# The second feed-forward product by seven half products per 512 inner rows

## The chip, the core and the metric

One core of one Trainium2 chip. The metric is the device time of one execution in microseconds (us): TensorE does matmuls, VectorE (DVE), ScalarE (ACT) and GpSimd (Pool) do the rest, SyncE (SP) issues the weight transfers. A run is timed several times and its median is given.

## What is computed

One decoder layer for 512 tokens of width 2048: two groups of linear-attention heads, then a feed-forward part (FF) of inner width 8192. Of the reference only the last lines matter here:

```python
h = rmsnorm(x, pre_ffn_norm[l]) * (1.0 + sc_f) + sh_f
y = jnp.square(jax.nn.relu(h @ w_ff1[l])) @ w_ff2[l]
x = x + gt_f * rmsnorm(y, post_ffn_norm[l])
```

All data are float32. `w_ff1` is 2048 x 8192, `w_ff2` is 8192 x 2048.

## The kernel before

**Split products.** Each float32 operand is split into a high part (a cast to the fp32r type, on ScalarE) and a low part (the difference, on VectorE, rarely on Pool). A product is three matmuls (`mm3`): high x high, high x low, low x high, all into one PSUM bank of 128x512.

**The weight stream.** `WeightStream` walks a `plan`, a list of weight tiles of 128x1024 in the order of their use. `_load` issues the transfer of a tile into one of three `raw` buffers; `_split` makes `wh` (L81) and `wl` (L83) in one of two buffers each; `get` returns the split tile that is due, after it has issued loads three tiles ahead and splits one tile ahead. `on_get` is called at each `get`; in the FF it advances, at every third call, `ada_gtf`, which loads 64 tiles of `w_ada`, scales them on ScalarE (L320) and adds them on Pool (L322) to `gacc2`, the gain of the last norm.

**The FF.** The 8192 inner columns are done in `NR` = 16 rounds of 512. `ff1(r)` computes the round's 512 inner columns, as four blocks of 128 inner columns (on partitions) by 512 tokens: 8 weight tiles, 24 matmuls each, 4 PSUM banks (`pf`), then relu, square, cast (`gH`) and difference (`gL`). `ff2(r)` multiplies them with 512 rows of `w_ff2`: for each of four column blocks `nb` of 512, two weight tiles (`hf`), four token blocks, each in a bank (`pg`) that collects 12 matmuls; VectorE then copies (first round, L1480) or adds (L1482) the bank into `y2` in SBUF. The order is `ff1(0)`, `ff1(1)`, `ff2(0)`, `ff1(2)`, `ff2(1)` and so on. Inside this loop the instruction order of TensorE and SyncE is as written (`manual_schedule`); that of VectorE, ScalarE and Pool is chosen by the compiler's scheduler. After the loop the gain is summed over partitions (`total_of`, banks `pgf`), and `ff2(NR - 1)` and the last norm follow, the last two column blocks in a token-by-token order written out by hand for all engines.

**PSUM.** Eight banks: three `pj` (for `pf`), two `wg`, and `wh`, `sg`, `sh`. `ff2` uses `wg`, `wg`, `wh`, `sg`.

```python
with tc.manual_schedule(engines={ET.PE, ET.SP}):
    for r in range(NR):
        ff1(r)
        if r >= 1:
            ff2(r - 1)
```

Of the kernel before, what the change touches and what calls it, by code (L numbers as in the profile page):

```python
# [45 lines left out]
class WeightStream:  # L46


    def __init__(self, nc, pool, plan, load_ahead, split_ahead, bufs):
# [7 lines left out]
        self.raw, self.hl = {}, {}  # L57

    def _load(self):
        i = self.nl  # L60
        raw = self.pool.tile([P, 1024], F32, tag="raw", name=f"raw{i}", bufs=self.bufs[0])
        ap = self.plan[i][1]
# [5 lines left out]
        self.raw[i] = raw  # L68
        self.nl += 1
        if self.on_load is not None:  # L70
            self.on_load(1.46)

    def _split(self):
        i = self.ns
        raw = self.raw.pop(i)
        pool, nb = self.pool, self.bufs
        if len(self.plan[i]) > 2:
            pool, nb = self.alt, (0, self.plan[i][2], self.plan[i][2])
        h = pool.tile([P, 1024], F32R, tag="wh", name=f"wh{i}", bufs=nb[1])
        lo = pool.tile([P, 1024], F32R, tag="wl", name=f"wl{i}", bufs=nb[2])  # L80
# [3 lines left out]
        ap = self.plan[i][1]  # L84
        k = 8 if isinstance(ap, list) else ap.shape[1]
        self.hl[i] = (
            h.rearrange("p (k n) -> p k n", k=k),
            lo.rearrange("p (k n) -> p k n", k=k),
        )
        self.ns += 1  # L90

    def get(self, key):
        i = self.ng
        assert self.plan[i][0] == key, (self.plan[i][0], key)
        n = len(self.plan)
        while self.nl < min(n, i + 1 + self.la):
            self._load()
            while self.ns < min(self.nl, i + 1 + self.sa):
                self._split()
        while self.ns < min(n, i + 1 + self.sa):  # L100
# [8 lines left out]
def hybrid_layer_kernel(  # L109
# [68 lines left out]

    def plan_f1(r):
        for g in range(RB // 2):  # L180
            for q in range(4):
                plan.append((("f1", r * RB * P + g * 256, q), w256(W1, r * RB * P + g * 256, q)))

    def plan_f2(r):
# [4 lines left out]

    for r in range(NR):  # L190
        plan_f1(r)
        if r >= 1:
            plan_f2(r - 1)
    plan_f2(NR - 1)
# [22 lines left out]
    ws = WeightStream(nc, wpool, plan, 3, 1, (3, 2, 2))  # L217
    ws.pool_l = range(LP0, LP1, LP2)


# [1197 lines left out]
    with ExitStack() as st:  # L1418
        fp = st.enter_context(tc.tile_pool(name="ff", bufs=1))
        y2 = big.tile([P, 4, D], F32, tag="y", name="y2")  # L1420
        gacc2 = fp.tile([P, D], F32, tag="gacc", name="gacc2")
        gH, gL = {}, {}

        def ada_gtf():
# [3 lines left out]
            for i in range(4 * KT + 2):  # L1428
# [4 lines left out]
                if i >= 2:  # L1433
                    cb, r = divmod(i - 2, KT)
                    ada_pool(queue.pop(0), 512, r, 1, gacc2[:, cb * 512 : (cb + 1) * 512], False)
                yield

        def ff1(r):
            gH[r] = fp.tile([P, RB, T], F32R, tag="gH", name=f"gH{r}", bufs=2)
            gL[r] = fp.tile([P, RB, T], F32R, tag="gL", name=f"gL{r}", bufs=2)  # L1440
            for g in range(RB // 2):
                col = r * RB * P + g * 256
                pss_ = [pj(f"pf{col}_{cb}") for cb in range(2)]
                for q in range(4):
                    wH, wL = ws.get(("f1", col, q))
                    for cb in range(2):
                        for kk in range(4):
                            kt = q * 4 + kk
                            cs = slice(cb * P, (cb + 1) * P)
                            mm3(pss_[cb], wH[:, kk, cs], wL[:, kk, cs], h2H[:, kt, :], h2L[:, kt, :],  # L1450
                                kt == 0, kt == KT - 1)
                for cb in range(2):
                    j = g * 2 + cb
                    rl = fp.tile([P, T], F32, tag="rl", name=f"rl{r}_{j}", bufs=2)
                    nc.scalar.activation(out=rl, in_=pss_[cb], func=AF.Relu)
                    sq = fp.tile([P, T], F32, tag="sq", name=f"sq{r}_{j}", bufs=2)
                    nc.scalar.activation(out=sq, in_=rl, func=AF.Square)
                    nc.scalar.copy(out=gH[r][:, j, :], in_=sq)
                    nc.vector.tensor_tensor(out=gL[r][:, j, :], in0=sq, in1=gH[r][:, j, :].bitcast(F32),
                                            op=ALU.subtract)  # L1460

        FB = ("wg", "wg", "wh", "sg")

        def ff2_mm(ps, r, tok, hf, w):
            ts = slice(tok * P, (tok + 1) * P)
            for jj in range(2):
                j = 2 * hf + jj
                mm3(ps, gH[r][:, j, ts], gL[r][:, j, ts], w[0][:, jj, :], w[1][:, jj, :], j == 0, j == RB - 1)

        def ff2(r, nbs=range(4)):  # L1470
            for nb in nbs:
# [5 lines left out]
                for tok in range(4):  # L1477
                    dst = y2[:, tok, nb * 512 : (nb + 1) * 512]
                    if r == 0:
                        nc.vector.tensor_copy(out=dst, in_=ps4[tok])  # L1480
                    else:
                        nc.vector.tensor_tensor(out=dst, in0=ps4[tok], in1=dst, op=ALU.add)  # L1482

# [8 lines left out]
        ws.on_get = on_get  # L1492
        with tc.manual_schedule(engines={ET.PE, ET.SP}):
            for r in range(NR):
                ff1(r)
                if r >= 1:
                    ff2(r - 1)


        Gf = big.tile([P, D], F32, tag="hL", name="Gf")  # L1500
        nc.sync.dma_start(out=Gf, in_=post_ffn_norm[0].partition_broadcast(P))
        for cb in range(4):
            cs = slice(cb * 512, (cb + 1) * 512)
            ps = pj(f"pgf{cb}")
            total_of(ps, gacc2[:, cs], fp.tile([P, T], F32R, tag="rl", name=f"gfH{cb}", bufs=2),
                     fp.tile([P, T], F32R, tag="sq", name=f"gfL{cb}", bufs=2))
            nc.vector.tensor_tensor(out=Gf[:, cs], in0=ps, in1=Gf[:, cs], op=ALU.mult)
# [5 lines left out]
        rsf = fp.tile([P, 4], F32, name="rsf")  # L1513
        junk = fp.tile([P, 512], BF16, name="junkf")

        ws.alt = fp

# [10 lines left out]

        zl = fp.tile([P, 512], F32, name="zl")

# [66 lines left out]
```

## Time and profile before

| | us |
|---|---|
| median of 3 runs | 2715.55 (2712.93 to 2716.62) |
| the profiled execution | 2714.78 |
| its span, first to last instruction | 2713.1 |
| TensorE busy | 2563.6 (94%) |
| VectorE busy | 1440.6 (53%) |
| ScalarE busy | 1016.4 (37%) |
| Pool busy | 569.9 (21%) |

The span has three parts: the start and the heads, until about 1100 us; the output projection and norms, until about 1310 us; the FF. In the trace a matmul is shown longer (0.39 us) than the distance to the next, since neighbours overlap; distances between starts are what to read. The same holds for short instructions of VectorE in a row.

### The profile page before, as it was taken

To read this page: it belongs to the slowest core of one execution; us is meant where nothing else is said; L and a number is where in the kernel's file an instruction comes from. 1 tells how busy PE (TensorE), PEld (TensorE's weight loads), DVE (VectorE), ACT (ScalarE), POOL (GpSimd) and SP (SyncE) were. 2 spreads that over 40 slices of the span, in tenths; PEclk is the share of its full clock that TensorE was granted. 3 is DMA by queue.
4 is the path that set the end of the run, shared out by engine and by line. 5 is a ranking of instruction groups with operands and counts; after the bars stand their busy time and mean duration, and the time that the engine had idled before them with its cause. 6 is when DMAs were issued, how large, how long until landed. Compare 5 with 4: busy or idle time off the path is not lost.

```text
span 2713.1 us, 34048 instructions
## 1 busy us (share of the span) xinstructions
PE 2563.6 (94%) x12987; PEld 2080.2 (77%) x12987; DVE 1440.6 (53%) x2265; ACT 1016.4 (37%) x1675; POOL 569.9 (21%) x496
## 2 busy tenths in 40 slices
PE   5889999999997789999999999999999999999997
PEld 3667777777775567788788888888888888888886
DVE  7997868776865366634533343334333344334346
ACT  5543554454543242433533233332233223322233
POOL 4560344544444340000100000000000000000003
PEclk8999999999998899999999999999999999999999
DMA  9974885778899985445233333333333333332342
GB/s 280 283 186 73 133 138 128 151 138 153 139 138 103 98 135 79 143 129 186 90 117 109 118 112 115 111 114 111 112 117 111 115 110 116 105 101 93 101 171 109
DMA packets 335938, 350.65 MB, mean 129 GB/s; under 512 B 17191, under 2 KB 255001, under 8 KB 334621
## 3 DMA queue, kind: packets, MB, share of 16 engines
q1 hardware_dynamic: 335578, 348.42, 53.8%
q8 instruction: 102, 1.67, 0.2%
q14 instruction: 62, 0.51, 0.1%
q10 hardware_dynamic: 196, 0.06, 0.0%
HBM read 340.01 MB, written 8.40 MB: 128 GB/s over the span
## 4 chain that ended last, share of the span: by engine, by line
PE 65%; DVE 5%; DMA 3%; issue 2%; POOL 1%; ACT 1%; SPq 0%; DVEq 0%; ACTq 0%; POOLq 0%
PE pf L203 25%; PE pg L203 25%; PE pj L203 7%; PE pout L203 6%; DMA raw<-in_w_in_dram 2%; DVE wl L83 1%; PE pa L203 1%; POOL y L1521 0%; POOL aacc L322 0%; DVE x2r L1539 0%; DVE uc L912 0%; DVE utmp L910 0%; PE p L203 0%; DVE zkT L364 0%; PE pz L203 0%
## 5 line engine op out<-in xcount | busy, mean ns | idle before, releaser
L83 DVE TENSOR_TENSOR wl<-raw,wh 128x1024 fp32r<-128x1024 f32 x418 | 525.4, 1258 | 827.3 <-ACT wh L81 821.0
L81 ACT CAST wh<-raw 128x1024 fp32r<-128x1024 f32 x424 | 445.9, 1052 | 1216.5 <-PE pg L203 477.9
L203 PE MATMUL pf<-h2L,wh 128*128 128x512 f32 x1024 | 399.2, 390 | 0.0
L203 PE MATMUL pf<-h2H,wh 128*128 128x512 f32 x1024 | 399.2, 390 | 0.0
L203 PE MATMUL pf<-h2H,wl 128*128 128x512 f32 x1024 | 398.9, 390 | 0.0
L203 PE MATMUL pg<-wh,gL 128*128 128x512 f32 x992 | 385.9, 389 | 0.0
L203 PE MATMUL pg<-wl,gH 128*128 128x512 f32 x992 | 385.9, 389 | 0.0
L203 PE MATMUL pg<-wh,gH 128*128 128x512 f32 x992 | 385.9, 389 | 0.0
L203 PE MATMUL pj<-hH,wh 128*128 128x512 f32 x768 | 328.9, 428 | 7.3 <-ACT wh L81 7.3
L322 POOL TENSOR_TENSOR aacc<-ada,aacc 128x512 f32<-128x512 f32 x180 | 268.5, 1492 | 256.7 <-ACT ada L320 222.7
L203 PE MATMUL pj<-hH,wl 128*128 128x512 f32 x768 | 308.2, 401 | 6.9 <-DVE wl L83 6.9
L203 PE MATMUL pj<-hL,wh 128*128 128x512 f32 x768 | 306.7, 399 | 0.0
L322 POOL TENSOR_TENSOR gacc<-ada,gacc 128x512 f32<-128x512 f32 x64 | 83.2, 1300 | 940.6 <-ACT ada L320 940.6
L203 PEld LDWEIGHTS pf<-h2L,wh 128*128 128x128 f32 x1024 | 192.5, 188 | 39.9
L203 PEld LDWEIGHTS pf<-h2H,wh 128*128 128x128 f32 x1024 | 192.5, 188 | 39.8
L203 PEld LDWEIGHTS pf<-h2H,wl 128*128 128x128 f32 x1024 | 192.4, 188 | 39.8
L203 PEld LDWEIGHTS pg<-wl,gH 128*128 128x128 f32 x992 | 186.2, 188 | 38.7
L203 PEld LDWEIGHTS pg<-wh,gH 128*128 128x128 f32 x992 | 186.2, 188 | 38.6
L203 PEld LDWEIGHTS pg<-wh,gL 128*128 128x128 f32 x992 | 186.2, 188 | 38.6
L1482 DVE TENSOR_TENSOR y<-pg,y 128x512 f32<-128x512 f32 x232 | 154.6, 687 | 70.7 <-PE pg L203 70.7
L203 PEld LDWEIGHTS pj<-hH,wl 128*128 128x128 f32 x768 | 148.0, 193 | 44.0 <-DVE wl L83 10.5
L203 PEld LDWEIGHTS pj<-hH,wh 128*128 128x128 f32 x768 | 148.5, 193 | 37.8 <-ACT wh L81 8.7
(411 smaller groups left out, 3346.3 us busy)
## 6 DMA issues: line engine op xcount, KB each, us to landing
raw<-in_w_ff_dram SPq DMA_DIRECT2D x256, 512.0 KB, 3.7
ada<-in_w_ada_dram SPq DMA_DIRECT2D x256, 256.0 KB, 7.9
raw<-in_w_in_dram SPq DMA_DIRECT2D x96, 512.0 KB, 9.4
adas<-in_w_ada_dram SPq DMA_DIRECT2D x128, 256.0 KB, 5.4
raw<-in_w_out_dram SPq DMA_DIRECT2D x40, 512.0 KB, 3.8
raw<-in_w_in_dram SPq DMA_DIRECT2D x40, 256.0 KB, 4.2
raw<-in_w_in_dram SPq DMA_DIRECT2D x48, 128.0 KB, 5.3
xo<-in_x_dram SPq DMA_DIRECT2D x8, 512.0 KB, 8.7
```

Of the source, the lines that this page charges most:

```text
L81: self.cast = self.nc.scalar.copy(out=h, in_=raw).ins
L83: eng.tensor_tensor(out=lo, in0=raw, in1=h.bitcast(F32), op=ALU.subtract)
L203: nc.tensor.matmul(ps, lhsT=lhsT, rhs=rhs, start=start, stop=stop)
L322: nc.gpsimd.tensor_tensor(out=acc, in0=a, in1=acc, op=ALU.add)
L1482: nc.vector.tensor_tensor(out=dst, in0=ps4[tok], in1=dst, op=ALU.add)
```

## The change

In rounds 0 to 14 the second product is done by Strassen's scheme on 2 x 2 blocks. A round has 512 inner rows, cut in two halves of 256; the 512 tokens are cut in two halves of 256; the columns of `w_ff2` are taken as pairs of blocks of 512, `m` and `m + 2`, for `m` = 0 and 1. Per round and `m` there are seven half products in the order 2, 6, 4, 1, 3, 7, 5, each 256 tokens x 256 inner rows x 512 columns: two banks of 6 matmuls (`ff2s`). What changes around them:

- `combos` makes, once a round on VectorE and ScalarE, the five sums or differences of activation blocks and the two plain blocks, as high and low parts (`cH`, `cL`, one buffer each); `ff1` leaves the squared activations in `gs[r]` in float32.
- `WeightStream._sum` makes five of the seven weight operands on Pool, each from two loaded tiles of 128x1024, three of them in place. `raw` gets three more buffers and `wh`/`wl` one more pair each, in the FF's own pool (`wide`); `get` then issues loads and sums two tiles ahead and more, and splits two tiles ahead.
- Each product is copied or added by VectorE into accumulators in SBUF: four are the quarters of `y2`, two (products 4 and 5) are in `m45`; product 1 is added to two of them. After round 14 `gather` combines the accumulators by 24 additions.
- Five banks are used in turn for `pg`. The two halves of `ff1` (`g` = 0, 1) now alternate with the two column groups: `ff1(r+1, 0)`, `ff2s(r, 0)`, `ff1(r+1, 1)`, `ff2s(r, 1)`; at the end `ff2s(14, 0)`, `ff2s(14, 1)`, `plain(0)`, `gather`, `ff1(15, 1)`, `plain(1)`.
- The last round stays as it was; `plain` makes its `gH` and `gL`. `ada_gtf` moves on at every fourth `get`, behind the last cast on ScalarE. Some small tiles share buffers with others.

The diff, cut to its core:

```diff
+    def _sum(self):
+        i = self.nsum
+        self.nsum += 1
+        if self.plan[i][0][0] != "s2":
+            return
+        a, op, b = self.plan[i][2]
+        if b is None:
+            return
+        ra, rb = self.raw[a], self.raw[b]
+        self.uses[a] -= 1
+        self.uses[b] -= 1
+        out = ra
+        if self.uses[a]:
+            self.uses[i] = 1
+            out = self._raw(i)
...
+        self.nc.gpsimd.tensor_tensor(out=out, in0=ra, in1=rb, op=op)
+        self.raw[i] = out
...
+        sa = self.sa if self.wide is None else 2
+        su = min(n, i + 1 + max(2, sa))
+        st = min(n, i + 1 + sa)
+        if self.wide is not None:
+            while self.nl < self.upto[su - 1]:
+                self._load()
+            while self.nsum < su:
+                self._sum()
+            while self.ns < st:
+                self._split()
-        while self.nl < min(n, i + 1 + self.la):
+        while self.nl < min(len(self.loads), self.upto[i] + self.la):
             self._load()
...
+    SEVEN = ((2, "11", None, None), (6, "11", ALU.add, "12"), (4, "21", ALU.subtract, "11"),
+             (1, "11", ALU.add, "22"), (3, "12", ALU.subtract, "22"), (7, "21", ALU.add, "22"),
+             (5, "22", None, None))
...
+        yield from ((1, 0, 0), (1, 0, 1))
+        for r in range(NR - 1):
+            last = r == NR - 2
+            yield from ((1, r + 1, 0), (2, r, 0))
+            yield from ((2, r, 1), (1, r + 1, 1)) if last else ((1, r + 1, 1), (2, r, 1))
...
+            for cb in range(2):
+                v = gs[r][:, cb, g, :]
+                nc.scalar.activation(out=v, in_=pss_[cb], func=AF.Relu)
+                nc.scalar.activation(out=v, in_=v, func=AF.Square)
+        def combos(r):
+            cH = fp.tile([P, 2, 7, 256], F32R, tag="cH", name=f"cH{r}")
+            cL = fp.tile([P, 2, 7, 256], F32R, tag="cL", name=f"cL{r}")
+            for jj in range(2):
+                S = fp.tile([P, 5, 256], F32, tag="gS", name=f"gS{r}_{jj}")
+                g4 = gs[r][:, jj].rearrange("p h (t n) -> p (h t) n", t=2)
+                nc.vector.tensor_tensor(out=S[:, 0:2, :], in0=g4[:, 0:2, :], in1=g4[:, 2:4, :], op=ALU.add)
+                nc.vector.tensor_tensor(out=S[:, 2:4, :], in0=g4[:, 1:3, :], in1=g4[:, 0::3, :], op=ALU.subtract)
+                nc.vector.tensor_tensor(out=S[:, 4, :], in0=g4[:, 0, :], in1=g4[:, 3, :], op=ALU.add)
+                nc.scalar.copy(out=cH[:, jj, 0:5, :], in_=S)
+                nc.vector.tensor_tensor(out=cL[:, jj, 0:5, :], in0=S, in1=cH[:, jj, 0:5, :].bitcast(F32),
+                                        op=ALU.subtract)
+                nc.scalar.copy(out=cH[:, jj, 5:7, :], in_=g4[:, 0::3, :])
+                nc.vector.tensor_tensor(out=cL[:, jj, 5:7, :], in0=g4[:, 0::3, :],
+                                        in1=cH[:, jj, 5:7, :].bitcast(F32), op=ALU.subtract)
+            cs_[r] = (cH, cL)
+        RING = ("wg", "wh", "wg", "sg", "sh")
...
+        def ff2s(r, m):
+            cH, cL = cs_[r]
+            for i, *_ in SEVEN:
+                wH, wL = ws.get(("s2", r, m, i))
+                for tb in range(2):
+                    ps = bank(RING[nps[0] % 5], f"pg{r}_{m}_{i}_{tb}")
+                    nps[0] += 1
+                    ts = slice(tb * P, (tb + 1) * P)
+                    for jj in range(2):
+                        mm3(ps, cH[:, jj, PLACE[i], ts], cL[:, jj, PLACE[i], ts], wH[:, jj, :], wL[:, jj, :],
+                            jj == 0, jj == 1)
+                    for dst, first in sums_of(i, m, tb):
+                        if r == 0 and first:
+                            nc.vector.tensor_copy(out=dst, in_=ps)
+                        else:
+                            nc.vector.tensor_tensor(out=dst, in0=ps, in1=dst, op=ALU.add)
+        def gather(m):
+            lo_, hi_ = slice(m * 512, (m + 1) * 512), slice(1024 + m * 512, 1024 + (m + 1) * 512)
+            for tb in range(2):
+                c11, c12, c21, c22 = y2[:, tb, lo_], y2[:, tb, hi_], y2[:, 2 + tb, lo_], y2[:, 2 + tb, hi_]
+                m4, m5 = m45[:, tb, lo_], m45[:, 2 + tb, lo_]
+                for dst, v, op in ((c11, m4, ALU.add), (c11, m5, ALU.subtract), (c22, c12, ALU.add),
+                                   (c22, c21, ALU.subtract), (c12, m5, ALU.add), (c21, m4, ALU.add)):
+                    nc.vector.tensor_tensor(out=dst, in0=dst, in1=v, op=op)
...
-            if pace["n"] % 3 == 0:
+            if pace["n"] % 4 == 0:
...
         with tc.manual_schedule(engines={ET.PE, ET.SP}):
-            for r in range(NR):
-                ff1(r)
-                if r >= 1:
-                    ff2(r - 1)
+            for kind, r, g in ff_order():
+                if kind == 1:
+                    ff1(r, g)
+                    if g == 1 and r == 0:
+                        combos(0)
+                    if r == NR - 1 and g == 1:
+                        plain(1)
+                else:
+                    ff2s(r, g)
+                    if g == 1 and r < NR - 2:
+                        combos(r + 1)
+                    elif g == 1:
+                        plain(0)
+                        gather(0)
+                        gather(1)
```

## Rows read from the trace of the kernel before

**Rows 1.** Page: busy by engine; busy tenths and granted clock in 40 slices.

```profile
PE 2563.6 (94%) x12987; PEld 2080.2 (77%) x12987; DVE 1440.6 (53%) x2265; ACT 1016.4 (37%) x1675; POOL 569.9 (21%) x496
...
PE   5889999999997789999999999999999999999997
...
DVE  7997868776865366634533343334333344334346
...
PEclk8999999999998899999999999999999999999999
```

**Rows 2.** Chain that ended last, in time: start, length, engine, tile, count.

```profile
1391.40 43.52 PE pg L203 x192
1434.92 43.52 PE pf L203 x192
...
2609.96 43.52 PE pg L203 x192
```

**Rows 3.** Table by windows: busy PE, PEld, DVE, ACT, POOL; clock, DMA, GB/s.

```profile
1400.00:1500.00 100.00, 100.00 (x443) 82.81 (x442) 38.90 (x44) 30.37 (x36) 8.14 (x7) 1.00 0.37 115
2400.00:2500.00 100.00, 100.00 (x443) 82.81 (x442) 35.16 (x38) 27.64 (x33) 0.00 (x0) 1.00 0.31 97
```

**Rows 4.** Who waited for whom, 1320:2640 us: total, times, longest.

```profile
POOL gacc L322 <- ACT ada L320: 940.6, 64, 16.9
DVE wl L83 <- ACT wh L81: 645.7, 243, 4.2
```

**Rows 5.** Groups by line and form, 1330:2640 us: busy, mean ns; idle before.

```profile
L83 DVE TENSOR_TENSOR wl<-raw,wh 128x1024 fp32r<-128x1024 f32 x241 | 295.3, 1225 | 644.2 <-ACT wh L81 644.2
L81 ACT CAST wh<-raw 128x1024 fp32r<-128x1024 f32 x241 | 254.3, 1055 | 819.6 <-PE pg L203 455.9 <-PE pf L203 363.7
...
L1482 DVE TENSOR_TENSOR y<-pg,y 128x512 f32<-128x512 f32 x217 | 144.6, 687 | 66.8 <-PE pg L203 66.8
L322 POOL TENSOR_TENSOR gacc<-ada,gacc 128x512 f32<-128x512 f32 x63 | 81.9, 1300 | 935.5 <-ACT ada L320 935.5
L320 ACT ACTIVATE ada<-ada,c 128x512 f32<-128x512 f32 x63 | 45.7, 725 | 27.0 <-DMA ada<-in_w_ada_dram 27.0
L1459 DVE TENSOR_TENSOR gL<-sq,gH 128x512 fp32r<-128x512 f32 x63 | 44.4, 705 | 104.4 <-ACT gH L1458 104.4
...
L1455 ACT ACTIVATE rl<-pf 128x512 f32<-128x512 f32 x62 | 36.8, 594 | 48.2 <-PE pf L203 48.2
```

**Rows 6.** Groups by line and form on Pool, 0:250 us.

```profile
L83 POOL TENSOR_TENSOR wl<-raw,wh 128x1024 fp32r<-128x1024 f32 x6 | 15.7, 2617 | 16.7 <-ACT wh L81 16.7
```

**Rows 7.** Waits of the DMA queue of SyncE, 1320:2640 us: total, times, longest.

```profile
SPq L66 <- DVE wl L83: 1165.2, 242, 5.2
```

**Rows 8.** VectorE in order of time: start, length, instruction, count, idle before.

```profile
1430.61 1.23 DVE L83 TENSOR_TENSOR wl<-raw,wh 128x1024 fp32r<-128x1024 f32 x1 [4.21 <-ACT wh L81]
1431.75 1.28 DVE L1480 COPY y<-pg 128x512 f32<-128x512 f32 x2
```

**Rows 9.** TensorE in order of time where the last gain is summed.

```profile
2655.14 0.50 PE L203 MATMUL pgf<-gfH,onesr 128*128 128x512 f32 x1
2655.48 0.40 PE L203 MATMUL pg<-wl,gH 128*128 128x512 f32 x1
```

**Rows 10.** VectorE in order of time, about 303 us.

```profile
302.53 1.65 DVE L83 TENSOR_TENSOR wl<-raw,wh 128x1024 fp32r<-128x1024 f32 x1 [0.64 <-ACT wh L81]
```

**Rows 11.** Pool in order of time, about 303 us.

```profile
300.45 2.66 POOL L322 TENSOR_TENSOR aacc<-ada,aacc 128x512 f32<-128x512 f32 x2 [3.40 <-ACT ada L320]
303.25 2.08 POOL L322 TENSOR_TENSOR aacc<-ada,aacc 128x512 f32<-128x512 f32 x1 [0.15 <-POOL aacc L322]
```

**Rows 12.** VectorE in order of time, about 90 us.

```profile
89.83 0.74 DVE L736 SCALAR_TENSOR_TENSOR ht<-pt,sc,R 128x512 f32<-128x512 f32 x1
90.49 1.95 DVE L311 SCALAR_TENSOR_TENSOR asum<-adas,c,asum 128x256 f32<-128x256 f32 x1
```

**Rows 13.** Pool in order of time, about 90 us.

```profile
89.74 2.42 POOL L83 TENSOR_TENSOR wl<-raw,wh 128x1024 fp32r<-128x1024 f32 x1
```

More of the change, by code (lines that the diff above doesn't have):

```diff
@@ L57, in __init__, with start, _raw @@
         self.raw, self.hl = {}, {}
+    def start(self):
+        self.loads, self.upto, self.uses = [], [], {}
+        for i, e in enumerate(self.plan):
+            if isinstance(e[0], tuple) and e[0][0] == "s2":
+                self.loads += e[1]
+                for k in e[2][0::2]:
+                    if k is not None:
+                        self.uses[k] = self.uses.get(k, 0) + 1
+            else:
+                self.loads.append((i, e[1]))
+                self.uses[i] = 1
+            self.upto.append(len(self.loads))
+        self.ring = []
+        self.nsum = self.nraw = self.nw = 0
+        self.wide = None
+    def _raw(self, key):
+        i = self.nraw
+        self.nraw += 1
+        pool, tag, nb = self.pool, "raw", self.bufs[0]
+        if self.wide is not None and i % 2:
+            pool, tag = self.wide, "raw2"
+        self.ring.append(key)
+        if self.wide is not None and len(self.ring) > 2 * nb:
+            old = self.ring.pop(0)
+            assert self.uses[old] == 0, (key, old)
+        return pool.tile([P, 1024], F32, tag=tag, name=f"raw{i}", bufs=nb)
     def _load(self):
-        i = self.nl
-        raw = self.pool.tile([P, 1024], F32, tag="raw", name=f"raw{i}", bufs=self.bufs[0])
-        ap = self.plan[i][1]
+        key, ap = self.loads[self.nl]
+        raw = self._raw(key)
         aps = ap if isinstance(ap, list) else [ap]
@@ L83, in _split @@
         eng.tensor_tensor(out=lo, in0=raw, in1=h.bitcast(F32), op=ALU.subtract)
-        ap = self.plan[i][1]
-        k = 8 if isinstance(ap, list) else ap.shape[1]
+        ap = e[1]
+        k = 2 if two else 8 if isinstance(ap, list) else ap.shape[1]
         self.hl[i] = (
@@ L218, in hybrid_layer_kernel @@
     ws.pool_l = range(LP0, LP1, LP2)
+    ws.start()
     ident = const.tile([P, P], F32, name="ident")
@@ L1434, in ada_gtf @@
                     cb, r = divmod(i - 2, KT)
-                    ada_pool(queue.pop(0), 512, r, 1, gacc2[:, cb * 512 : (cb + 1) * 512], False)
+                    ada_pool(queue.pop(0), 512, r, 1, gacc2[:, cb * 512 : (cb + 1) * 512], False, ws.cast)
                 yield
[L1438 to L1451, printed above, removed]
-                for cb in range(2):
[L1453 to L1460, printed above, removed]
@@ new lines, in plain @@
+        def plain(g):
+            r = NR - 1
+            if g == 0:
+                gHL.append(fp.tile([P, RB, T], F32R, tag="cH", name="gH"))
+                gHL.append(fp.tile([P, RB, T], F32R, tag="cL", name="gL"))
+            for cb in range(2):
+                j = 2 * g + cb
+                nc.scalar.copy(out=gHL[0][:, j, :], in_=gs[r][:, cb, g, :])
+                nc.vector.tensor_tensor(out=gHL[1][:, j, :], in0=gs[r][:, cb, g, :],
+                                        in1=gHL[0][:, j, :].bitcast(F32), op=ALU.subtract)
```

114 lines of the change are left out of this document (87 added, 27 removed).

## The prediction

> **What bounds the kernel now.** I read the page first: TensorE is busy for 94% of the span, and the second half of the 40 slices shows a full nine in the PE row with the clock at full speed, and VectorE, the busiest of the others, at three to six [rows 1]. The chain of work that ended last then says what that means: from 1391 us to 2610 us it is nothing but matmuls, in 29 pieces of 43.52 us and 192 matmuls, one FF2 round (`pg`) and one FF1 round (`pf`) in turn; the first two and the last are shown [rows 2]. 43.52 / 192 = 0.2267 us per matmul, without a gap. The reader should also see that the `pf` piece closes 4 PSUM banks and the `pg` piece 16, and both take 43.52 us: changing banks costs TensorE nothing. In the same stretch the table by windows has PE at 100 us of 100, VectorE at 35 to 39, ScalarE at 28 to 30, Pool at 0 to 8 and the DMA engines at about a third [rows 3]. Who waits for whom agrees: the longest waits are of Pool for ScalarE and of VectorE for ScalarE, and no wait of PE is in the list [rows 4]. So in this stretch a matmul fewer is 0.2267 us less, until another engine falls behind.
>
> **What is removed.** Before, one FF2 round is 16 banks of 12 matmuls. After, in 15 of 16 rounds, it is 2 column groups x 7 products x 2 token blocks x 6 matmuls = 168. That is 24 fewer in each of 15 rounds, 360 in all: 360 x 0.2267 = 81.6 us. The last round stays plain. The Trainium skill ("TensorE: Matmul & The Clock Gate", Back-to-back issue gap) gives N/2.4 + 2.5 ns, 216 ns for 512 columns; by that the removal would be 360 x 0.216 = 77.8 us. The trace's 0.2267 is measured on this very form, so I keep 81.6.
>
> **What is added, per round of 512 inner rows, beside TensorE.** The round becomes 192 + 168 = 360 matmuls, 81.6 us, instead of 87.0.
> VectorE: the low parts `wl` go from 16 to 22 (8 for FF1, 14 for the products), 1.225 us each [rows 5]: 27.0 us. PSUM results added to SBUF go from 16 to 32 of 0.687 us (product 1 goes into two accumulators and the other six into one, per token block): 22.0 us. The sums of activations and their low parts are per half 2 operations of 512 columns and one of 256, one low part of 1280 and one of 512; priced by the 0.705 of `gL`, half of that for 256, and 1.25 x 1.225 for 1280, they are 4.0 us, twice a round 8.0. The four `gL` of 0.705 go away. Total 57 us of 81.6, 70%, against 33.4 of 87 before. That is not the bound over a round.
> ScalarE: 22 casts of 1.055 us, 4 relus and 4 squares of some 0.6 as now, casts of the activation sums about 3.7 us instead of 2.1 (by 1.055 per 1024 columns), and some 5 `ada` scalings of 0.725 [rows 5]: about 36 of 81.6 us.
> Pool: 10 sums of 128x1024 per round. The trace has this very shape on Pool, 2.617 us, six times in the start phase [rows 6]: 26.2 us, with the `ada` additions of 1.300 us (one per four weight tiles, some 5 a round) about 33 us of 81.6.
> DMA: the same weight bytes as before, in tiles of the same shape; a third of the DMA engines' time is used [rows 3]. The queue's own list has one wait that matters, for `wl` to free a raw tile [rows 7]; there will be 6 raw tiles instead of 3. Cost: nothing; the cover is that a raw tile is asked for several products before it is used (walk below), and if that cover were gone each late tile would cost up to a transfer.
>
> **A half-round walked through.** Take the start of an FF1 half as 0. Four weight tiles of 5.44 us (24 matmuls) run to 21.76, seven products of 2.72 us to 40.8. There are three pairs of `wh`/`wl`, so the cast for a tile can begin when TensorE has finished the third before it, and has two tiles' time: 5.44 us inside the products, against 1.06 + 1.23 of work, so some 3.1 us of slack. A raw tile is free six allocations later. Going round that ring, all four quarter tiles of a column group have been asked for by 8 us (22 last, after the split of FF1's fourth tile), that is 14 us before the first product. The sums on Pool: 11+12 about 0, 21-11 at 3.4, and the three that write over a loaded tile (11+22, 12-22, 21+22) must wait for the split of product 2's tile at about 13.3 and then run one behind another to about 21.1. Product 1, the first that needs one of those three, has its cast at 24.5. So Pool's work falls beside FF1 matmuls, and VectorE has only four `wl` there (and the activation sums every second time, about 8 us of work with ScalarE between, in time for a `wl` due at 10.9).
> Inside the seven products VectorE has 16 additions and 7 `wl` in 19.04 us. Back to back an eviction of a bank occupies 0.60 us and a `wl` 1.14: two evictions together take 1.28, the second of them shown as long as ever, and the first starts 1.14 after the `wl` [rows 8]. That is 9.6 + 8.0 = 17.6 of 19.04 us. It is tight, 92%, but five banks in turn let an addition come 4 x 1.36 = 5.4 us late. The worst product is the one with four additions, 2.4 + 1.14 = 3.5 against 2.72: 0.8 us behind, made up in the two after it. I price what still leaks (a relu ahead of a cast, one `ada` addition on Pool beside a `wl`) at 0.1 us per half-round, 30 of them: 3 us; bounds 0 and, by the rivals below, 2 us each.
>
> **The two ends.** Before the last FF1 half, the accumulators are combined: 24 additions of 512 columns on VectorE, 0.60 each back to back, 14.4 us, beside 21.76 us of FF1 matmuls. But they are written ahead of the split of that half's third tile, due at 10.9 us. Some can go earlier (the first column group is complete one block before), the rest end at 11 to 16 us, then `wl`: TensorE stands for 0 to 6 us. I take 4, since few gaps of VectorE are free in that block. The kernel's tail keeps its work; today the matmuls of the last gain (`pgf`) are dealt in between those of FF2 as they get ready [rows 9], so that the later freeing of their tiles need not hold up TensorE: 0, with -2 to +3.
>
> **Sum.** The profiled execution took 2714.8 us, its span 2713.1. 2714.8 - 81.6 + 3 + 4 + 0 = 2640.2. The median of the runs is 0.8 above that execution: 2641.
>
> **Rivals.**
> Locked weights. `wl` and Pool's addition shut each other out [rows 10, 11]: `wl` starts at 302.53, Pool's second addition ends at 303.11, and `wl` ends at 304.18, so it took its usual time only from there (1.65 instead of 1.23); the next Pool addition, begun at 303.25, then lasted 2.08 instead of 1.30. The long Pool operation does the same: a VectorE operation with two SBUF inputs, begun at 90.49, lasts 1.95 us, until Pool's 2.42 us are over, while the one with a PSUM input begun at 89.83, beside the same Pool operation, keeps 0.74 [rows 12, 13]. For this kernel: additions from PSUM are not shut out, but each `wl` that meets a sum waits up to 2.6 us, and the additions behind it in VectorE's queue wait too. If one sum a half-round slips into the products, 17.6 + 2.6 = 20.2 exceeds 19.04 by 1.2, and with a late cast 1 to 2 us are lost: 30 x 1 to 2 = 30 to 60, so 2664 to 2694. For it: 92%. Against it: the walk puts four of five sums wholly before the products. The Trainium skill ("SBUF — State Buffer", SBUF: two separate sides) states the same as an exclusive lock held for a whole instruction; by that rule the time is that of this rival if the sums come late, and the trace agrees (1.65 and 2.08 above).
> Slower. The order on Pool and VectorE isn't written out by hand here (only that of PE and SP is). If it puts the sums among the products, k of them a half-round, VectorE needs 17.6 + 2.62k in 19.04 us, and 3.1 us can be late without harm: the loss is 2.62k - 4.5. The gain is 81.6 / 30 = 2.72 a half-round. The decision lies between two and three sums: with three, 3.3 x 30 = 100 us, so 2734; with four, 2812. For it: raw tiles freed late would delay all the sums. Against it: 14 us in hand.
> It doesn't do what it says. If the shorter runs of 6 matmuls per bank cost TensorE something, the gain goes: 0.45 us for each of 14 banks and the time is that of before, about 2715. Against it speaks that 4 and 16 banks take the same time [rows 2].
>
> **How the numbers follow.** Forecast (2632 to 2655) 0.62; locked weights (2655 to 2700) 0.22; slower 0.11; gain eaten up in part or whole, by either of the last two, 0.05 (0.02 still faster, 0.03 the same). The range from 2632 (all of the gain and 2 us of the tail) to 2692 leaves out about 0.2. A measurement of this kernel can tell 0.2%, 5.4 us, from no change. So faster 0.86, same 0.03, slower 0.11.
>
> **What would show it.** In the chain after: `pf` pieces of 43.52 us a round and `pg` pieces of 168 x 0.2267 = 38.1 us; any more is leak. PE's waits should be short and for `wl` at one place, the last FF1 half (0 to 6 us); waits for the additions mean VectorE's queue. The sums on Pool should lie between products and start of the next, at 2.4 to 3.7 us each; `wl` in the products should stay near 1.23 us and not show 2.3 or more. VectorE should be at some 70% of a round. I am wrong if PE waits every half-round.

## The result, and the profile after

The changed kernel takes 2674.7 us (median of four runs, 2674.3 to 2675.8), the kernel before, on the same chip, 2714.2 us: ratio 0.9854, 95% interval 0.9837 to 0.9871. Later runs of the same file gave 2672.2 us and 0.9855 (0.9841 to 0.9870). The time lies in the range of 2632 to 2692 us, 34 us above the forecast of 2641. The gain is 39.5 us where 74.6 were forecast. The span of the profiled execution is 2672.8 us, and the prediction's sum, taken to the span, was 2638.5.

The page of the changed kernel, busy time and tenths, against [rows 1]:

```profile
PE 2497.4 (93%) x12627; PEld 2020.5 (76%) x12627; DVE 1870.6 (70%) x2709; ACT 1119.4 (42%) x1765; POOL 1036.3 (39%) x646
...
PE   5889999998996779999999999999999999999998
...
DVE  7997868766764538553647668777778676777796
```

360 matmuls are gone, as counted. VectorE is about twice as busy in the second half (mostly 7 tenths where it was 3 to 4), and Pool's busy time has nearly doubled over the run (569.9 to 1036.3 us). The chain that ended last, in time, against [rows 2]:

```profile
1400.87 19.04 PE pg L307 x84
1419.91 21.76 PE pf L307 x96
```

Half a round of FF1 is 21.76 us and one column group 19.04, together 40.80 or 81.6 a round, where it was 87.04. From 1400.87 to 2543.27 us this goes on without a gap: 1142.4 us are 28 times 40.80, and no wait of TensorE is in the list for that stretch. So the steady state gives the whole gain, and what is missing lies outside it. The windows of two groups and of two FF1 halves (columns: busy PE, PEld, DVE, ACT, POOL; clock, DMA, GB/s), against [rows 3]:

```profile
1400.87:1419.91 19.04, 19.04 (x86) 15.77 (x85) 17.11 (x22) 8.98 (x10) 2.33 (x2) 1.00 0.49 170
1441.67:1460.71 19.04, 19.04 (x86) 15.77 (x85) 17.79 (x23) 9.68 (x12) 2.60 (x2) 1.00 0.50 167
1419.91:1441.67 21.76, 21.76 (x98) 18.02 (x97) 9.19 (x8) 6.21 (x8) 15.79 (x6) 1.00 0.26 84
1460.71:1482.47 21.76, 21.76 (x98) 18.02 (x97) 14.52 (x14) 9.39 (x12) 15.89 (x6) 1.00 0.24 73
```

VectorE is busy 17.1 and 17.8 of 19.04 us in the products, and TensorE is at 100% in all four. Pool's sums lie in the FF1 halves; what it does in the products are additions of `ada`. Pool in order of time there:

```profile
1419.99 2.41 POOL L120 TENSOR_TENSOR raw<-raw,raw 128x1024 f32<-128x1024 f32 x1 [7.45 <-DMA raw<-in_w_ff_dram]
1422.35 2.28 POOL L427 TENSOR_TENSOR gacc<-ada,gacc 128x512 f32<-128x512 f32 x1
1424.59 2.41 POOL L120 TENSOR_TENSOR raw<-raw,raw 128x1024 f32<-128x1024 f32 x1
1432.08 8.78 POOL L120 TENSOR_TENSOR raw<-raw,raw 128x1024 f32<-128x1024 f32 x3 [5.08 <-DMA raw<-in_w_ff_dram]
```

Counted from the start of the FF1 half (1419.91), the five sums run at 0.1, 4.7 and, three in a row, from 12.2 to 20.95 us. Over the whole steady stretch 132 of 143 sums start among FF1 matmuls. The groups over 1320 to 2600 us, against [rows 5]:

```profile
L154 DVE TENSOR_TENSOR wl<-raw,wh 128x1024 fp32r<-128x1024 f32 x334 | 492.3, 1474 | 309.8 <-ACT wh L152 305.1 <-DMA raw<-in_w_ff_dram 4.2
L120 POOL TENSOR_TENSOR raw<-raw,raw 128x1024 f32<-128x1024 f32 x150 | 433.4, 2905 | 409.1 <-DMA raw<-in_w_ff_dram 243.7 <-DVE wl L154 135.2 <-issue 21.8
...
L1607 DVE TENSOR_TENSOR y<-pg,y 128x512 f32<-128x512 f32 x344 | 219.0, 681 | 0.0
```

A low part `wl` (the texts below also call it a remainder) takes 1474 ns in the mean, 250 more than before; an addition from PSUM is as it was.

**Where 41.3 us went.** Before, the span was 2713.1; less 81.6 that is 2631.5, and 2672.8 is 41.3 above it. Three stretches hold it:

- *Ahead of the FF, 21.6 us.* The output projection `pout`, the last large product before the FF, starts later (first start behind the min/median/max of ns; before, then after):

```profile
L203 PE MATMUL pout<-wh,oH x256: 389/389/500, 1102.5 to 1285.5; 128*128 128x512 f32 x128
```

```profile
L307 PE MATMUL pout<-wh,oH x256: 389/389/506, 1124.1 to 1307.9; 128*128 128x512 f32 x128
```

- *The start of the FF, 9.6 us.* Going back from the first product's start by the FF1 matmuls ahead of it, the FF of before begins at 1391.40 - 2 x 43.52 = 1304.36, of after at 1400.87 - 3 x 21.76 = 1335.59: 31.2 later, of which 21.6 are told above. TensorE waits 6.63 us in it. ScalarE and TensorE there:

```profile
1343.35 1.04 ACT L152 CAST wh<-raw 128x1024 fp32r<-128x1024 f32 x1 [1.34 <-POOL h2L L1518]
1347.49 1.05 ACT L152 CAST wh<-raw 128x1024 fp32r<-128x1024 f32 x1 [3.10 <-DMA raw<-in_w_ff_dram]
```

```profile
1344.44 0.79 PE L307 MATMUL pf<-h2H,wh 128*128 128x512 f32 x1 [6.63 <-ACT wh L152]
```

TensorE has done 48 matmuls of the FF, two weight tiles, when it waits. The cast for the third tile (the expectation below calls it the second) is released by the norm's last step (`h2L`): that tile is split into the third pair (`wh2`, `wl2`), and this pair lies in memory that the norm still holds. The next cast then waits for a transfer that was asked for only at 1343.40 us.

- *The end, 10.1 us.* From the end of the last steady matmul (2653.48 before; after, 2543.27 + 38.08 + 21.76 = 2603.11 without gaps) to the end of the span it was 59.6 us and is 69.7. VectorE and TensorE in the last block:

```profile
2556.13 2.64 DVE L154 TENSOR_TENSOR wl<-raw,wh 128x1024 fp32r<-128x1024 f32 x1
...
2563.24 2.89 DVE L154 TENSOR_TENSOR wl<-raw,wh 128x1024 fp32r<-128x1024 f32 x1
...
2600.05 0.68 DVE L1617 TENSOR_TENSOR y<-y 128x512 f32<-128x512 f32 x1
2600.65 1.21 DVE L154 TENSOR_TENSOR wl<-raw,wh 128x1024 fp32r<-128x1024 f32 x1
```

```profile
2566.18 0.50 PE L307 MATMUL pg<-wl,cH 128*128 128x512 f32 x1 [0.93 <-DVE wl L154]
...
2601.91 0.80 PE L307 MATMUL pf<-h2H,wl 128*128 128x512 f32 x1 [4.43 <-DVE wl L154]
```

Two column groups stand in a row there, the sums of the second run among the products of the first, `wl` takes 2.2 to 2.9 us, and the 14 products of the block (28 banks) end at 2584.3 instead of 2581.35. Then 21 of the gather's 24 additions (L1617) run ahead of the `wl` at 2600.65, and TensorE waits 4.43 us for it. So the 10.1 us are 3.0 in the products and 8.9 in the last FF1 half (that wait and the lower clock behind it, told below), less 1.8 by which the rest is shorter than before.

The sum is 21.6 + 9.6 + 10.1 = 41.3. The theory to test: the last two are the change's own doing, at two places; the first is of another kind.

### The profile page after: what moved, and what is told of

Read it like the earlier page. It is cut to its first block, busy times and chain, and to the rows that moved or that the text cites. A ratio compares the mean times of both kernels' runs of the same rounds, so it can differ in the third digit from the quotient of the medians.

```text
span 2672.8 us, 34309 instructions
## 1 busy us (share of the span) xinstructions
PE 2497.4 (93%) x12627; PEld 2020.5 (76%) x12627; DVE 1870.6 (70%) x2709; ACT 1119.4 (42%) x1765; POOL 1036.3 (39%) x646
## 4 chain that ended last, share of the span: by engine, by line
PE 62%; DVE 6%; DMA 5%; issue 2%; ACT 1%; POOL 1%; SPq 0%; DVEq 0%; POOLq 0%; ACTq 0%
PE pf L307 26%; PE pg L307 21%; PE pj L307 7%; PE pout L307 6%; DMA raw<-in_w_in_dram 4%; DVE wl L154 1%; DMA ada<-in_w_ada_dram 1%; PE pa L307 1%; DVE y L1617 0%; POOL y L1703 0%; DVE y L1607 0%; POOL aacc L427 0%; DVE x2r L1721 0%; PE p L307 0%; ACT wh L152 0%
## 5 line engine op out<-in xcount | busy, mean ns | idle before, releaser
L154 DVE TENSOR_TENSOR wl<-raw,wh 128x1024 fp32r<-128x1024 f32 x506 | 717.7, 1419 | 504.3 <-ACT wh L152 497.4
L152 ACT CAST wh<-raw 128x1024 fp32r<-128x1024 f32 x512 | 538.5, 1052 | 1016.6 <-PE pf L307 283.1
L120 POOL TENSOR_TENSOR raw<-raw,raw 128x1024 f32<-128x1024 f32 x150 | 433.4, 2905 | 409.1 <-DMA raw<-in_w_ff_dram 243.7
L307 PE MATMUL pg<-wl,cH 128*128 128x512 f32 x840 | 327.4, 390 | 1.7 <-DVE wl L154 1.6
L307 PE MATMUL pg<-wh,cL 128*128 128x512 f32 x840 | 326.8, 389 | 0.0
L307 PE MATMUL pg<-wh,cH 128*128 128x512 f32 x840 | 326.8, 389 | 0.0
L427 POOL TENSOR_TENSOR gacc<-ada,gacc 128x512 f32<-128x512 f32 x64 | 117.4, 1834 | 268.1 <-issue 187.7
L1607 DVE TENSOR_TENSOR y<-pg,y 128x512 f32<-128x512 f32 x344 | 219.0, 681 | 0.0
L307 PEld LDWEIGHTS pg<-wl,cH 128*128 128x128 f32 x840 | 157.7, 188 | 36.3 <-DVE wl L154 3.7
L307 PEld LDWEIGHTS pg<-wh,cH 128*128 128x128 f32 x840 | 157.7, 188 | 32.8
```

The lines of the kernel that those rows point to most:

```text
L120: self.nc.gpsimd.tensor_tensor(out=out, in0=ra, in1=rb, op=op)
L307: nc.tensor.matmul(ps, lhsT=lhsT, rhs=rhs, start=start, stop=stop)
L427: nc.gpsimd.tensor_tensor(out=acc, in0=a, in1=acc, op=ALU.add)
L1607: nc.vector.tensor_tensor(out=dst, in0=ps, in1=dst, op=ALU.add)
```

## Experiments

Starts of `pout` are given with each run, because they differ from program to program; from there to the end of the span the two kernels took 1610.6 us (before) and 1548.7 us (after).

**Both kernels again**, unchanged.

> The changed kernel once more, untouched. In its first profile the whole front (everything ahead of the FF) ended 22 us later than in the kernel before: the output projection began at 1124.1 us against 1102.5 us, and the difference grew between 756 and 990 us, where the DMA engines are the bound. Theory A (nothing of the change, the transfers of one execution): a second profile moves this start by itself; it lies anywhere between 1095 and 1130 us, and by at least 5 us away from 1124. Theory B (the change costs 22 us in front, by a way not yet seen): it lies again within 3 us of 1124, and the untouched kernel before within 3 us of 1102. The time should be 2674.7 us again within 0.2%.

> The kernel before once more, untouched, for the same question: does the output projection begin at 1102.5 us again (theory B: the front of 22 us belongs to the change), or does its start vary from profile to profile by 5 us or more (theory A: it is the run of the transfers)? The time should be 2714 us within 0.2% either way, if the variation is inside one program's executions less than that; if A holds and the median of the runs stays put, the variation is one of programs on this chip and not of executions.

```profile
L307 PE MATMUL pout<-wh,oH x256: 388/389/502, 1126.2 to 1309.4; 128*128 128x512 f32 x128
```

```profile
L203 PE MATMUL pout<-wh,oH x256: 388/389/506, 1099.8 to 1282.5; 128*128 128x512 f32 x128
```

The first row is the changed kernel's, the second that of before; the medians were 2672.2 and 2713.2 us. The starts moved by 2.1 and -2.7 us and kept their distance (26.4 instead of 21.6): theory A falls, the delay goes with the program. What its transfers did, in the DMA view of 800 to 1000 us (packets, MB, share of the 16 DMA engines' time), first of before, then of after:

```profile
q1 hardware_dynamic: 27973, 22.58, 97.5%
```

```profile
q1 hardware_dynamic: 24644, 20.02, 94.6%
```

A packet took 0.975 x 16 x 200 / 27973 = 112 ns before and 0.946 x 16 x 200 / 24644 = 123 ns after, of the same tensors in the same sizes. The same working gives 112 to 113 ns in all four profiles of the kernel before and its variants below, and 121 to 125 ns in all ten of the changed kernel and its variants. SyncE's queue shows the two programs side by side until then; the first of these rows is of before, the second of after:

```profile
749.24 0.38 SPq L66 DMA_DIRECT2D raw<-in_w_in_dram  x1
```

```profile
749.39 1.62 SPq L94 DMA_DIRECT2D raw<-in_w_in_dram  x1
```

The same transfer is issued 0.15 us apart, and the queue of the changed kernel takes it 1.24 us more slowly. Up to the first matmul of the output projection the two traces list the same 960 instructions of SyncE with the same semaphores, and on the other engines the same operations on tiles in the same order.

**Own weight buffers later.** The third pair of split tiles and the FF's own raw ring come into use after the first half-round.

```
-        ws.wide = fp
-        ws.nraw, ws.ring = 0, []
 ...
                     ff1(r, g)
+                    if (r, g) == (0, 0):
+                        ws.wide = fp
+                        ws.nraw, ws.ring = 0, []
```

> One edit to the changed kernel: the FF's own additional weight buffers (the third pair of split tiles and the FF's own ring of raw tiles) come into use only after the first half-round, not from its first tile on. Theory (the start): in the changed kernel the second tile's split waits until the norm ahead of the FF has left the memory that these buffers take over, and its three raw transfers leave only then; this makes the start of the FF 9.2 us dearer than before, with a gap of 7.0 us in TensorE. Then this edit takes the gap away: 5 to 9 us faster, 2666 to 2670 us. Rival (the start is late by the transfers of the queue as a whole, and the memory is only the last of several waits): the gap goes elsewhere and the time stays within 2 us of 2674.7.

2663.8 us (2662.0 to 2664.2), ratio 0.9821 (0.9805 to 0.9838). `pout` starts at 1122.3 and the rest takes 1538.0 us, 10.7 less. The chain:

```profile
1333.21 56.24 PE pf L307 x248
```

248 FF1 matmuls at 0.2267 without a gap: the 9.6 us at the start of the FF come from the memory that the new buffers take over. SyncE asks for the next weight tile at 1329.97 us instead of 1343.40. The time fell by more than the 5 to 9 us expected. Worked out as above, 9.6 of the 10.7 us are gained at the start, the term that was missing; the other 1.1 come at the end, where the 46 matmuls behind the gather's wait took 12.12 us instead of 13.20.

**Gather last.** `gather(0)` and `gather(1)` move behind `plain(1)`, so behind the splits of the last FF1 half.

```
                     if r == NR - 1 and g == 1:
                         plain(1)
+                        gather(0)
+                        gather(1)
 ...
                         plain(0)
-                        gather(0)
-                        gather(1)
```

> One edit to the changed kernel: the 24 additions that gather the six accumulators come after the last FF1 half and its splits, not between the last block of Strassen products and that half. Theory (the gather is in the way): they are 24 ops of about 0.6 us on VectorE (13.3 us from first to last) ahead of the last half's weight remainders, and TensorE stands 4.8 us behind them; moved behind, the time falls by 4 to 6 us, to about 2669 to 2671 us. Rival (the next thing in VectorE's order is late as well, since the plain product's accumulations need the gathered sums): the gap moves behind the half and the time stays within 1.5 us of 2674.7.

2666.8 us (2664.4 to 2668.1), ratio 0.9831 (0.9816 to 0.9845). `pout` at 1120.2, then 1542.1 us, 6.7 less. The table by windows has no gap left around that half:

```profile
2575.00:2607.00 32.00, 31.92 (x142) 26.08 (x141) 31.00 (x44) 12.67 (x17) 0.00 (x0) 1.00 0.49 179
```

TensorE 31.92 of 32 us, with VectorE at 31.00: the additions slip in between. The gain is a little more than the 4 to 6 us expected. Of the 6.7 us, 6.2 come at the end and 0.5 at the start of the FF. So 6.2 of the 10.1 us at the end were the gather's place. Of the 3.9 that are left, 2.8 are the products of the last block, which still end late (2579.8 instead of 2577.0), and some 1 us lies behind them.

**Column groups in a row in every round**, as in the last block alone until now.

```
-            yield from ((1, r + 1, 0), (2, r, 0))
-            yield from ((2, r, 1), (1, r + 1, 1)) if last else ((1, r + 1, 1), (2, r, 1))
+            if last:
+                yield from ((1, r + 1, 0), (2, r, 0), (2, r, 1), (1, r + 1, 1))
+            else:
+                yield from ((1, r + 1, 0), (1, r + 1, 1), (2, r, 0), (2, r, 1))
```

> One edit to the changed kernel: in every round both FF1 halves come first and then both column groups of the Strassen products, as they do in the changed kernel in the last block alone; no half of FF1 lies between two groups of seven products. Theory (the alternation is what hides the sums): five Pool sums of 2.9 us per group then fall among products, their split remainders are slowed by them, and each of the 14 further rounds loses what the last block lost, about 3.1 us in its products (and the splits queued behind up to as much again): 14 x 3.1 = 43 us, 2718 us, between 2700 and 2750. Rival (the last block is dear by what follows it, not by its order): steady pieces of 21.76 and 19.04 us without a gap as before, 2674.7 us within 5.

2701.8 us (2701.0 to 2703.2), ratio 0.9954 (0.9937 to 0.9970): 27 us dearer. `pout` at 1120.5, then 1579.8 us, 31.1 more, or 2.2 in each of 14 rounds. The chain and the group of `wl` over 1390 to 2540 us:

```profile
1460.58 43.52 PE pf L309 x192
...
1544.32 43.52 PE pf L309 x192
```

```profile
L154 DVE TENSOR_TENSOR wl<-raw,wh 128x1024 fp32r<-128x1024 f32 x300 | 496.2, 1654 | 299.6 <-ACT wh L152 299.6
```

The round shown is 83.74 us and not 81.6. FF1 runs as ever; the loss is in the products, where `wl` meets Pool's sums: 70 of the 139 sums of this stretch start among products (11 of 143 in the changed kernel), a `wl` that starts there takes 1678 ns in the mean (1277), and all 35 waits of TensorE are for `wl`. The theory holds in kind; its 3.1 us a round was too much, since the last block, from which it was taken, is dearer than the others.

**Sums on VectorE.** `nc.gpsimd.tensor_tensor` becomes `nc.vector.tensor_tensor` in `_sum`.

> One edit to the changed kernel: the ten weight sums of a round run on VectorE and not on Pool. Theory (in the steady state TensorE is the bound with slack in VectorE, so it doesn't matter who sums): VectorE was busy 58 to 62 of 82 us; ten sums at 1.2 to 2.0 us add 12 to 20 us, and without Pool's sums beside them the remainders fall from 1474 to about 1225 ns, which takes 22 x 0.25 = 5 us away; 65 to 77 of 82 us, TensorE still without a gap, and the time stays within 4 us of 2674.7. In the last block the sums among the products no longer slow the remainders, up to 3 us faster there. Rival (VectorE in the products is full, 92% by the prediction's walk): sums and remainders in one engine's order leave TensorE waiting 1 to 3 us in each of 30 half-rounds, 2705 to 2765 us.

2676.8 us (2671.9 to 2679.7), ratio 0.9860 (0.9845 to 0.9874); `pout` at 1127.8, then 1550.1 us, 1.4 more. The chain, and two groups over 1390 to 2540 us:

```profile
1404.55 19.04 PE pg L307 x84
1423.59 21.76 PE pf L307 x96
```

```profile
L154 DVE TENSOR_TENSOR wl<-raw,wh 128x1024 fp32r<-128x1024 f32 x310 | 386.6, 1247 | 133.6 <-ACT wh L152 133.4
...
L120 DVE TENSOR_TENSOR raw<-raw,raw 128x1024 f32<-128x1024 f32 x142 | 182.5, 1322 | 60.0 <-DMA raw<-in_w_ff_dram 59.6
```

Without Pool's sums `wl` is back at 1247 ns, and a sum costs 1322 ns instead of 2905. TensorE has no gap in either kernel. VectorE is busy 67.0 of 81.6 us in a round. So in the steady state neither Pool nor VectorE sets the time; Pool's help is worth nothing here, and the slower `wl` costs nothing.

In the last block the expectation failed: no `wl` is slowed there, and yet nothing is gained. The sums now stand in VectorE's own order among the products, each of the five between two low parts. One of them on VectorE, and the wait of TensorE for the `wl` ahead of it:

```profile
2573.95 1.23 DVE L154 TENSOR_TENSOR wl<-raw,wh 128x1024 fp32r<-128x1024 f32 x1
2575.09 1.22 DVE L120 TENSOR_TENSOR raw<-raw,raw 128x1024 f32<-128x1024 f32 x1
```

```profile
2575.23 0.50 PE L307 MATMUL pg<-wl,cH 128*128 128x512 f32 x1 [0.54 <-DVE wl L154]
```

The block's products end at 2587.7 instead of 2585.0, 2.7 us late, where the changed kernel loses 3.0. So what costs there is that five sums fall among products, by either engine; the lock is one way in which it costs.

**Both edits together.**

> The two edits together, the FF's own weight buffers taken into use after the first half-round and the gather after the last FF1 half. Measured from the start of the output projection to the end of the profile the changed kernel took 1548.7 and 1548.8 us, the first edit alone 1538.0 (10.7 less), the second alone 1542.1 (6.7 less). Theory (two separate places): the gains add up, 17.4 us less, 1531.4 us from that start to the end, and about 2657 us in all. Rival (both gaps are one queue that catches up later): less than 12 us in sum, over 1537 us.

2660.4 us (2656.8 to 2661.7), ratio 0.9799 (0.9784 to 0.9814), faster than either kernel. `pout` at 1121.8, then 1533.2 us, 15.5 less; 17.4 were expected, and the rival (under 12) falls. The gains are 9.4 us at the start of the FF and 6.1 at the end. Most of what is missing was counted twice: the 1.1 us that the first edit alone gained behind the gather's wait, which is gone here, and the 0.5 that the second alone gained at the start, which the first takes whole. Of 81.6 us, 1610.6 - 1533.2 = 77.4 are now kept behind the front.

**Buffers later, and the last block alternates too.** The order `(1,r+1,0), (2,r,0), (1,r+1,1), (2,r,1)` holds for every round; `gather(0)` follows (2,14,0), and `plain(0)`, `plain(1)`, `gather(1)` follow (2,14,1).

> The first edit (own weight buffers later), and the last block's order alternates like all the others: FF1 half, products, FF1 half, products. The first group's gather follows its products, the last half's splits and the second gather follow the second group's products. Theory (the two column groups in a row cost 3.1 us in the products, and the gather 4.8 us ahead of the last half): both go, but the splits of the last half (four casts and four remainders of 0.7 us) now lie between the last Strassen product and the plain product, a gap of 3 to 5 us; in sum 1530 to 1536 us from the start of the output projection to the end, against 1538.0 with the first edit alone and 1531.4 expected of the two edits. Rival (the plain product's accumulations wait for the gather in its new place as well): a gap of 5 to 10 us, and no gain over 1538.

2660.6 us (2658.7 to 2666.0), ratio 0.9805 (0.9790 to 0.9820). `pout` at 1127.6, then 1536.3 us: 1.7 better than the first edit alone, 3.1 behind both edits, and just over the 1530 to 1536 expected. In the products of the last block TensorE now waits for nothing, and they end on time: the 3.0 us there came from the two column groups in a row. The row that is late comes after:

```profile
2615.71 0.80 PE L305 MATMUL pg<-wh,gH 128*128 128x512 f32 x1 [3.65 <-DVE y L1646]
```

TensorE waits 3.65 us for an accumulation (L1646) of the plain product, which comes in VectorE's order behind the second gather, the sums of the last gain and two splits: a gap of the rival's kind, smaller than the 5 to 10 us that it said.

**A longer program, and more memory**, both for the front. Behind the end, 3000 memsets of one column on Pool; or a further tensor of 25.6 MB in the chip's memory, of which four columns are written.

> The kernel before, with 3000 memsets of one column on Pool behind its end; ahead of them nothing is changed, so the time is longer by whatever these take and says nothing: what is read is the start of the output projection (1102.5 and 1099.8 us in two profiles of the kernel before, 1120 to 1128 us in eight profiles of the changed kernel and of its variants, though the instructions ahead of it are the same ones in the same order with the same semaphores). Theory P (where a program of another size puts things in memory sets the pace of the weight transfers): the start moves by 10 us or more, towards 1120. Theory N (it hangs on something else): it stays between 1099 and 1103 us.

> The changed kernel with the same 3000 memsets of one column on Pool behind its end, for the same question; the time says nothing. Theory P: the start of the output projection moves by 10 us or more from the 1120 to 1128 us of the changed kernel and its variants, back towards 1101. Theory N: it stays between 1118 and 1130 us. If neither of the two longer programs moves its start, what makes the front later stays open.

> The kernel before, with a further tensor of 25.6 MB in the chip's memory, of which four columns are written behind the end (a few us); ahead of that nothing is changed. The program's own tensors took 4.3 MB until now, so what the runtime lays behind them may come to lie elsewhere. Read is the start of the output projection (1099.8 to 1104.0 us in three profiles of the kernel before and of its longer program). Theory M (where the tensors lie in memory sets the pace of the transfers of w_in between 756 and 990 us): it moves by 8 us or more. Theory N (it hangs on something else): it stays between 1098 and 1106 us.

> The changed kernel with the same further tensor of 25.6 MB, for the same question. Theory M: the start of the output projection moves by 8 us or more away from the 1120 to 1128 us of the changed kernel and its variants, or comes to lie with the kernel before and the same tensor within 5 us. Theory N: it stays between 1118 and 1130 us, and then what makes the front of the changed kernel later stays open, since the instructions ahead of it are the same.

Their `pout` rows, in this order:

```profile
L203 PE MATMUL pout<-wh,oH x256: 388/390/505, 1104.0 to 1287.4; 128*128 128x512 f32 x128
```

```profile
L307 PE MATMUL pout<-wh,oH x256: 388/390/504, 1123.4 to 1306.1; 128*128 128x512 f32 x128
```

```profile
L203 PE MATMUL pout<-wh,oH x256: 389/389/500, 1101.1 to 1284.2; 128*128 128x512 f32 x128
```

```profile
L307 PE MATMUL pout<-wh,oH x256: 389/389/506, 1120.5 to 1303.2; 128*128 128x512 f32 x128
```

The memsets make the time 3166.9 and 3123.4 us, the tensor 2714.0 and 2668.9 us (one run each). Against the first profile of the same kernel none of the starts moved by more than 4 us; 1104.0 is 1 us outside the range that theory N gave, and far from the 10 us of theory P. The kernel before begins `pout` at 1099.8 to 1104.0 us in four profiles, the changed kernel and its variants at 1120.2 to 1127.8 in ten. So neither a longer program on Pool nor 25.6 MB more of the program's own memory moves the start towards that of the other kernel. A longer program on another engine, and where the weights themselves lie, were not tried; the cause stays open.

## Why the prediction was right and wrong

**Right.** The removal: 360 x 0.2267 = 81.6 us, seen whole in the steady pieces (81.6 a round, 87.04 before). The load of the other engines: VectorE 57 of 81.6 us forecast, 58.6 measured (the sum of the four windows); ScalarE 36 and 34.3; Pool 33 and 36.6. The walk: VectorE at 17.6 of 19.04 us in the products, measured 17.1 and 17.8; the three late sums from 13.3 to 21.1, measured 12.2 to 20.95. In the rows shown a landing transfer releases these three (5.08 us of waiting), and not the split that the walk named. So 92% of VectorE was enough, and the leak of 3 us is 0: what was still late fitted the slack. The third rival falls too: 84 matmuls in 14 banks took 19.04 us, 0.2267 each, so runs of 6 to a bank cost nothing. Its price was also mis-sized: 0.45 us holds for each of the 12 banks that a round has more than before (28 against 16), and for each of a half-round's 14 it would be 2.72 / 14 = 0.19.

**In the range by luck.** The median of 2674.7 us lies in the range, but outside the forecast's own part of it (2632 to 2655, chance 0.62). It lies where the rival of the locked weights was put (2655 to 2700, chance 0.22), and that rival's loss, 1 to 2 us in each half-round, didn't occur. What filled the 34 us are three terms outside the steady state, the front, the start of the FF and its end, of which the sum had 4 us. The forecast was right about the steady rounds; that the total came to lie in the range is no merit of its reasons.

**Locked weights.** The mechanism of this rival is real, and acts where it said. The Trainium skill ("SBUF — State Buffer", SBUF: two separate sides) has an exclusive lock between a VectorE operation with two SBUF inputs and a Pool operation that reads SBUF. The runs agree: `wl` takes 1247 ns without Pool's sums, 1474 with them, 1654 with half of them among the products, and an addition from PSUM 676 to 682 in any case. The alternating order, however, keeps the sums out of the products, as the walk had it, so the price is 0 in the steady state. Where the order doesn't alternate, sums among products cost 2.2 us a round, and some 3 us in the last block, to which the walk was not applied. The rule of the "slower" rival, 2.62 us for each sum among the products, was too hard. For two groups in a row with five sums it gives 2 x 17.6 + 5 x 2.62 - 38.08 - 3.1 = 7.1 us; 2.2 were measured, since a `wl` that meets a sum is prolonged by less than a whole sum (2.2 to 2.9 us instead of 1.23 in the rows of the last block).

**Wrong, the start of the FF: 0 taken, 9.6 us measured.** The part on DMA said that the raw tiles were asked for several products ahead, which holds in the steady state. It didn't ask what the new buffers cover: memory of the phase before, which the first tiles must wait for. The term was missing; the first edit took these 9.6 us away.

**Wrong in size, the end: 4 us taken, 10.1 measured.** The mechanism was named (24 additions ahead of a split, 0 to 6 us), and the wait of 4.43 us is near the 4 taken. The sum had nothing for what follows a wait: the granted clock was 0.50 from 2602 to 2605 us, that is the lower level, and 0.87 in the mean until 2614. Moving the gather gave 6.2 at this end. It also had nothing for the last block's own products, 3.0 us late because two column groups stand in a row there; with the alternating order they end on time.

**Wrong, the front: 0 taken, 21.6 us measured.** The sum has no term for the front; it takes it as unchanged without saying why. The instructions there are the same, and the time isn't. It is tied to the program and shows as slower transfers (112 against 123 ns a packet) in the stretch where the DMA engines are busy for 95 to 98% of the time; why they are slower stays open. This is the largest of the three terms.

In sum: 2638.5 + 21.6 (front) + 9.6 (start) + 6.1 (end) - 3 (leak) = 2672.8.

## What to carry to other kernels

Price the first and the last round apart from the steady one: a walk through a round says nothing on what its buffers must wait for at the start, or on a block whose order is another. Where new buffers are put into memory that the phase before still uses, let the first tiles keep their old ones. And compare two kernels from a common point in the trace, not by their ends alone, since a stretch in which no instruction differs can still move.

## What the hardware showed that was not expected

Transfers of identical instructions took 10% longer a packet in one program than in another (123 and 112 ns), with `pout` later in every profile, and two changes outside that stretch didn't alter it. Behind a wait of 6.63 us TensorE was at a granted clock of 0.50, the lower of its two levels, in the row below (it had 1.00 from 1325 to 1337), and behind the 4.43 us it was the same, with matmuls 0.43 us apart instead of 0.23. So a gap costs more than its length:

```profile
1344.40:1347.60 3.20, 3.12 (x7) 2.01 (x8) 1.23 (x1) 0.11 (x1) 1.17 (x1) 0.50 0.97 304
```

VectorE at 93% (17.8 of 19.04 us) with a low part `wl` in each product left TensorE without one gap in 28 half-rounds.
